# Where the halves of an output weight are made: beside the sample attention, or during the gates and back through DRAM

## The chip, the cores and the metric

The kernel runs on one core of a Trainium2 chip. Five engines work side by side, each from its own queue of instructions: TensorE (PE; its weight loads are listed apart as PEld), VectorE (DVE), ScalarE (ACT), GpSimd (POOL) and SyncE (SP), which here issues nearly all DMA transfers. The metric is the time of one execution on the device in microseconds, the median over runs.

## The reference

One inference step of a two-layer decoder. Layer 0 is a Mamba-2 mixer, layer 1 is multi-head latent attention (MLA), and a norm follows. A prompt of 1024 tokens goes through both. So do 8 sample sequences of 8 new tokens, whose attention also reads 2048 cached positions each, kept in pages of 128 positions that a page table points to. All is in float32. The parts that matter here:

```
def latent_partial(q_lat, q_pe, ckv, kpe, mask):
    s = (jnp.einsum('bqhc,bkc->bhqk', q_lat, ckv.astype(F32))
         + jnp.einsum('bqhr,bkr->bhqk', q_pe.astype(F32), kpe.astype(F32))) * MLA_SCALE
    ...
    m = jnp.max(s, axis=-1)
    p = jnp.exp(s - m[..., None])
    return m, jnp.sum(p, axis=-1), jnp.einsum('bhqk,bkc->bhqc', p, ckv.astype(F32))

def mla_output(o, gate, w_out):
    b, t = o.shape[:2]
    gated = o.reshape(b, t, MLA_WIDTH) * jax.nn.silu(gate.astype(F32))
    return jnp.einsum('bte,ed->btd', gated.astype(gate.dtype), w_out)
...
y_prompt = rms_norm(hp, final_norm_w)
```

`kpe` are the rotary keys of a cached position (32 numbers), `ckv` its latent (256 numbers). `w_out` of the second layer is a matrix of 1024 by 1024; it is the weight that the change is about.

## The kernel before, in words

**Halves.** A float32 product is made of three faster ones: each operand is held as a high half (a copy rounded to the type float32r) and a low half (the operand minus the high half). `split` makes them: a copy on ScalarE, then a subtraction on VectorE or GpSimd (lines 127 to 133).

**The order of the work.** The program is written as Python generators that are stepped in turn. A scheduler then orders each engine's instructions by its own simulated times, so an instruction can be put earlier in its queue than where it is written, as far as its data and buffers allow; `issue_after(x)` puts an instruction behind `x` in the queue of `x`'s engine. In the last two stages the order on TensorE and GpSimd is as written.

**Stages of the second layer.** `mla_in` projects the 1088 tokens. It begins with the gates: eight blocks of 128 columns (`gate_block`), each made of three products (`proj_piece`) of 24 matmuls into one of two PSUM buffers `pj`; ScalarE takes each product out with a SiLU (line 972) and SP stores the block to DRAM. Beside the gates, `gather_kpe` transposes and splits the cached rotary keys and stores the halves to DRAM (two stores of 2 MB, line 1526). Then come keys and latents (`mla_kv`) and queries (`mla_cq`, `mla_q`).

`mla_heads` is the prompt's attention, head by head. During the last head it also starts the sample attention, whose generator `Sample.flow` handles 32 page groups ("pages" from here on), four for each of the eight sequences. One page is 128 rows of 1024 numbers, 512 KB, fetched by GpSimd with an indirect DMA four pages ahead (`load`, line 1625); its rotary rows come in sets for two pages (`load_tk`, three DMAs on SP, line 1618, two buffers). For a page the flow does: two transposes of the page (`turn`, line 1690, with copy and subtraction on lines 1693 and 1694); the scores (seven matmuls, the last one with the rotary rows `tk`); maximum, scale and exponential (lines 1636, 1641, 1644); the transposed probabilities (`turn_p`, line 1732); the halves of the page (line 1703 on ScalarE, line 1705 on GpSimd); and the values (twelve matmuls into `o`), added to the running sum `ac` (line 1753). A new sequence begins with its new tokens (`first_scores`, tiles `P41n`, `pt41n`).

`mla_sample` takes the flow over after the heads, from page 2 on, and beside it runs the output projection of the prompt, `MlaOut.pieces`: eight token tiles, each 48 matmuls with the weight `w5` (line 98). They are stepped from the flow as filler: page 8 does the first twelve matmuls, page 9 the next twelve, and so on (`OUT0`). For each tile an activation tile `og` is loaded from DRAM and split (lines 127 and 131), and a row block `h` is loaded to be added.

**The weight.** It is cut into eight slices of 128 rows, 512 KB each, used in the order `WORD`. Two raw slices are loaded in the last head (`preload`, line 1583), three more when the heads are done, and the last three as raw buffers come free (line 1875). Their halves are made within the flow, at pages 2 to 7 (`WSP`): a copy of 128 by 1024 on ScalarE (line 1883) and four subtractions of 128 by 256 on GpSimd or VectorE by turns (`WENG`, line 1887), each placed behind a named step of the page.

Of the kernel before, what the change touches and what calls it, by code (L numbers as in the profile page):

```python
# [315 lines left out]
def load_w(k, pool, src, nk, ncol, tag, bufs=3, raws=None, rbufs=2, eng=None, sub=0, late=None):  # L316
    raw = load_raw(raws or pool, nk, ncol, rbufs)
    k.nc.sync.dma_start(raw, src.rearrange("(k p) e -> p k e", p=128))
# [646 lines left out]


def gate_block(k, wp, raws, b):
    ws = kslices(load_w(k, wp, k.I["mla_w_in"][0][:, 800 + 128 * b : 928 + 128 * b], 8, 128, "wg", 3, raws, eng=k.nc.gpsimd, sub=4), 8)
    gt = wp.tile([128, T], F32, tag="gt", name=f"gt{b}", bufs=2)

    def ev(ci, t0, n, p):
        k.nc.scalar.activation(gt[:, t0 : t0 + n], p[:, :n], AF.Silu)
# [18 lines left out]
def mla_in(k, right, mid):  # L991
    tc, nc, I = k.tc, k.nc, k.I
    k.g_d = k.dram.tile([8, 128, T], F32, name="g_d")
    with ExitStack() as st:
# [3 lines left out]

        rw = st.enter_context(open_pool(tc, name="rw", bufs=1))
        sg = ExitStack()  # L1000
        wg = sg.enter_context(open_pool(tc, name="wpg", bufs=1))
# [31 lines left out]
        wcq = load_cw(k, wq, rw, 0, 512, "cw")  # L1033
        mla_kv(k, sp, wkv)
        wk.close()
# [5 lines left out]

def mla_kv(k, sp, ws):
    nc, I = k.nc, k.I
# [7 lines left out]
    for i, (t0, m) in enumerate(TILES):  # L1051
# [39 lines left out]
        if i < 8:  # L1091
            kh, kl = k.kT
            split(k, kh[64:96, t0 : t0 + m], kl[64:96, t0 : t0 + m], p[64:96, 256 : 256 + m])


# [363 lines left out]
def mla_heads(k, hd, sm, early, st):  # L1459
# [8 lines left out]
    for h in range(MH):  # L1468
        units, b = [], iter(())
        if h == MH - 2:  # L1470
            early.close()
            hd.rope_queries()
            sm.begin(st, hd.psum)
        if h + 1 < MH:
            a, b = hd.maxpass(h + 1, 0), hd.maxpass(h + 1, 1)
            units += [a] * 4 + [b, a, b, b, b, a] + [b] * 5
        if h + 2 < MH:
            g = hd.prep(h + 2)
            units = merge(units, [g] * hd.units(h + 2))
        if h + 2 == MH:  # L1480
            g = sm.prefetch()
            units[PF:PF] = [g] * 2
            units += [g] * 2
        if h + 1 == MH:
            flow = sm.flow()
            units = [flow] * FLOW
        total, done = len(units), 0
        for t in range(12):
            qc, jb = (0, t) if t < 4 else (1, t - 4)
            held.append((h, qc, jb, *hd.qk(h, qc, jb)))  # L1490
            if t == 0:
                step(turn)
                turn = b
            while done < total * (t + 1) // 12:
                step(units[done])
                done += 1
            if h + 1 == MH and t == 0:
                sm.preload()
            if len(held) > LEAD:
                hd.pv(*held.pop(0))  # L1500
# [44 lines left out]
class Sample:  # L1545
# [28 lines left out]

    def preload(self):
        k = self.k
        self.pre = ExitStack()
        pp = self.pre.enter_context(open_pool(k.tc, name="pre4", bufs=1))
        self.wraw = {}
# [20 lines left out]
    def late_open(self, st):  # L1600
        self.pre.close()
        ap = st.enter_context(open_pool(self.k.tc, name="ap4", bufs=1))
# [9 lines left out]
    def load_tk(self, n):  # L1612
        k, nc = self.k, self.k.nc
        tk = self.ep.tile([96, 4, 256], F32R, tag="tk", name=f"tk{n}", bufs=2)
        for j in range(3):
            src = k.kpe_d[j % 2][:, :, 128 * n : 128 * n + 256].rearrange("r c x -> c r x")
            with k.tc.issue_after(k.lastq.ins):
                nc.sync.dma_start(tk[32 * j : 32 * j + 32].bitcast(F32), src)
        for j in range(2):
# [13 lines left out]
    def softmax(self, name, s, n, old):  # L1633
# [6 lines left out]
        else:  # L1640
            self.nmi = nc.vector.tensor_scalar(nm, mx, -SCALE, old, op0=ALU.mult, op1=ALU.min)
        P = self.sp.tile([128, n], F32, tag=f"P4{n}", name=f"P4{name}", bufs=2)
# [42 lines left out]
    def turn(self, n, c):  # L1685
# [6 lines left out]
        tl = self.ep.tile([128, 512], F32R, tag=f"cTl{c}", name=f"cTl{n}_{c}", bufs=2)  # L1692
        a = nc.scalar.copy(th, pt)
        b = nc.vector.tensor_tensor(tl, pt, th.bitcast(F32), op=ALU.subtract)
        if self.out:
            self.out.pins = a, b
        self.cT[n, c] = (th, tl)
# [85 lines left out]
    def flow(self):  # L1783
        N = len(self.items)
        for n in range(-1, N + 1):
# [9 lines left out]
            if t:  # L1795
                self.turn(n + 1, 1)
                yield
            parts = [WORD[WSP.index(n) + x] for x in range(WSP.count(n))] if out else []
            for kk in parts:
                out.weight_split(kk, 0)  # L1800
            if 0 <= n < N:
                self.scores(n)
                self.weigh(n)
            if parts:
                out.pins = out.pins[0], self.nmi
            for kk in parts:
                out.weight_split(kk, 1)
            if n % 4 == 3 and t:
# [19 lines left out]
            if out:  # L1828
                if n in MORE:
                    next(out.fill, None)  # L1830
                if n + 1 == OUT0[0]:
                    next(out.fill)
                    self.k.nc.sync.dma_start(out.fw, self.k.I["final_norm_w"].partition_broadcast(128))
            yield


def mla_sample(k, sm, flow):
    with ExitStack() as st:
        psum = st.enter_context(open_pool(k.tc, name="ps4", bufs=1, space=PS))
        out = MlaOut(k, st, psum)  # L1840
        sm.open(st, psum, out)
        out.raw = sm.wraw
        for kk in WORD[2:5]:
            out.weight(kk)
        out.fill = fill = out.pieces(range(8))
        next(fill)
        for _ in flow:
            if not hasattr(sm, "accT") and not any(kk in out.raw for kk in WORD[:2]):
                sm.late_open(st)
        last = None  # L1850
# [11 lines left out]
class MlaOut:  # L1862
    def __init__(self, k, st, psum):
        tc, nc, I = k.tc, k.nc, k.I
# [3 lines left out]
        self.fw = sp.tile([128, D], F32, name="fw")  # L1868
        self.raw = {}
        self.ws = [[self.wp.tile([128, D], F32R, name=f"w5{x}{kk}", bufs=1) for x in "hl"] for kk in range(8)]  # L1870

    def weight(self, kk):
        k, nc, wp = self.k, self.k.nc, self.wp
        self.raw[kk] = self.sp.tile([128, D], F32, tag="h5", name=f"w5r{kk}", bufs=3)
        WQ(nc).dma_start(self.raw[kk], k.I["mla_w_out"][0][kk * 128 : kk * 128 + 128])

    def weight_split(self, kk, half):
        hi, lo = self.ws[kk]
        raw = self.raw[kk]
        nc, x = self.k.nc, WENG[WORD.index(kk)]  # L1880
        if not half:
            with self.k.tc.issue_after(self.pins[0].ins):
                nc.scalar.copy(hi, raw)
        for a in range(2 * half, 2 * half + 2):
            s = slice(256 * a, 256 * a + 256)
            with self.k.tc.issue_after(self.pins[1].ins):
                (nc.gpsimd if x & 2 else nc.vector).tensor_tensor(lo[:, s], raw[:, s], hi[:, s].bitcast(F32),
                                                                  op=ALU.subtract)
        if half:
            del self.raw[kk]  # L1890
            if 2 <= WORD.index(kk) < 5:
                self.weight(WORD[WORD.index(kk) + 3])

    def pieces(self, tiles, src=None):
        k, nc, sp, ws = self.k, self.k.nc, self.sp, self.ws

        def load(i):
# [15 lines left out]
        for n, i in enumerate(tiles):  # L1913
            t0, m = TILES[i]
            oh, ol, _, o2 = queue.pop(0)
            h = sp.tile([128, D], F32, tag="h5", name=f"h5{i}", bufs=3)
            nc.sync.dma_start(h[:m], k.h_d[t0 : t0 + m])
            if n + 1 < len(tiles):
# [5 lines left out]
            for hf, c in enumerate(cs):  # L1924
# [3 lines left out]
                for j, _ in enumerate(mm_tok(nc, p, m, nw, [  # L1928
                        (oh[:, kk], ol[:, kk], o2[:, kk], ws[kk][0][:, c], ws[kk][1][:, c]) for kk in WORD])):
                    if j == (7 if src else 11) and nw == 512:  # L1930
# [138 lines left out]
```

## Time and profile before

| | us |
|---|---|
| three runs | 1940.17, 1943.87, 1943.55 |
| median | 1943.55 |
| the profiled execution, its own time | 1941.21 |
| its span, first to last instruction | 1939.4 |
| TensorE busy | 1895.6 |
| VectorE / ScalarE / GpSimd busy | 1192.2 / 1109.9 / 837.5 |
| DMA moved | 202.02 MB, 104 GB/s on the mean |

The time is the slowest core's, and there is one core. Busy times come from one profiled execution; the 1.8 us between its time and its span lie around the first and last instruction. "Busy" for TensorE is modelled and says that a matmul was under way, not that it ran at full rate: the granted clock is a column of its own, 1.00 when nothing is held back. In the names of rows, `out<-in` are the program's tiles; `w5p`, `w5r` are raw slices of the weight, `w5h`, `w5l` its halves.

### The profile page before, as it was taken

Reading aid. Unit: us, or ns where it says so; the run is one execution under the profiler, and the core shown is the slowest. Engines: PE = TensorE matmul, PEld = TensorE weight load, DVE = VectorE, ACT = ScalarE, POOL = GpSimd, SP = SyncE. Lnnn points to the kernel's source line nnn. Section 1 sums busy time; section 2 is a strip of 40 time slices with the busy share of each in tenths; the row PEclk is TensorE's granted clock in tenths of the full one; section 3 lists DMA queues with packets and bytes.
Section 4 is the critical chain, followed back from the end, with each engine's and each line's share of the span. In section 5 each row is a group of like instructions: output and inputs, shape, how many; then the busy total and the mean of one; then the engine's idle time right before and its main releaser. Section 6 shows DMA issues by size and latency. Waiting matters only on the chain.

```text
span 1939.4 us, 33638 instructions
## 1 busy us (share of the span) xinstructions
PE 1895.6 (98%) x12023; PEld 1730.3 (89%) x12023; DVE 1192.2 (61%) x2501; ACT 1109.9 (57%) x2535; POOL 837.5 (43%) x1122
## 2 busy tenths in 40 slices
PE   9999999999999999899999999999999999899998
PEld 7999999999999999788787998898888888788887
DVE  5567666656666666765533104476887888766674
ACT  6467666666666676732214314336777777855552
POOL 2446565555655555443003212103443334764551
PEclk9999999999999999999999999999999999989999
DMA  5123323332323332544433333133111112654431
GB/s 168 47 72 89 98 82 94 83 108 85 97 81 96 86 93 88 193 157 159 179 116 118 123 152 94 56 107 96 47 51 41 51 41 59 215 167 155 156 128 39
DMA packets 181087, 202.02 MB, mean 104 GB/s; under 512 B 18828, under 2 KB 147608, under 8 KB 180536
## 3 DMA queue, kind: packets, MB, share of 16 engines
q1 hardware_dynamic: 175864, 180.08, 30.1%
q0 software_dynamic: 4976, 19.66, 3.0%
q8 instruction: 95, 1.56, 0.3%
q14 instruction: 72, 0.59, 0.1%
q10 hardware_dynamic: 80, 0.13, 0.0%
HBM read 146.52 MB, written 53.28 MB: 103 GB/s over the span
## 4 chain that ended last, share of the span: by engine, by line
PE 88%; DVE 3%; DMA 3%; ACT 3%; issue 1%; POOL 1%; SPq 0%; POOLq 0%; DVEq 0%; ACTq 0%
PE pj L86 21%; PE pz L98 9%; PE pq L98 6%; PE pob L98 5%; PE p L98 5%; PE poa L98 4%; PE py L636 3%; PE sc L86 3%; PE o L86 2%; PE sc L1369 2%; PE o L1432 2%; PE o L1434 2%; PE st L1401 2%; PE st L1402 2%; PE st L1403 2%; PE o L1433 2%
## 5 line engine op out<-in xcount | busy, mean ns | idle before, releaser
L86 PE MATMUL pj<-xh,wih 128*128 128x384 f32 (+1 forms) x768 | 254.2, 335 | 0.9 <-ACT xh L273 0.5
L86 PE MATMUL pj<-xl,wih 128*128 128x384 f32 (+1 forms) x768 | 254.0, 331 | 0.0
L86 PE MATMUL pj<-xh,wil 128*128 128x384 f32 (+1 forms) x768 | 253.2, 330 | 0.0
L1415 POOL TENSOR_TENSOR tl<-P,th 128x384 fp32r<-128x384 f32 (+1 forms) x96 | 90.6, 944 | 232.5 <-ACT P L1413 190.9
L526 DVE SCALAR_TENSOR_TENSOR acc<-raw,vec,acc 128x1112 f32<-128x1112 f32 x96 | 141.6, 1476 | 25.9 <-ACT acc L522 24.9
L86 PEld LDWEIGHTS pj<-xh,wih 128*128 128x128 f32 x768 | 143.9, 188 | 2.5 <-ACT xh L273 1.1
L86 PEld LDWEIGHTS pj<-xl,wih 128*128 128x128 f32 x768 | 144.5, 188 | 1.0
L86 PEld LDWEIGHTS pj<-xh,wil 128*128 128x128 f32 x768 | 144.4, 188 | 0.5
L98 PE MATMUL pz<-wih,xh 128*128 128x256 f32 x504 | 142.9, 287 | 0.9 <-ACT z L567 0.8
L98 PE MATMUL pz<-wil,xh 128*128 128x256 f32 (+1 forms) x504 | 140.4, 285 | 0.9 <-DVE wil L133 0.9
L1412 ACT ACTIVATE th<-st 128x512 fp32r<-128x512 f32 x192 | 94.6, 493 | 66.0 <-PE st L1408 50.3
L631 ACT ACTIVATE M<-M,tok 128x128 f32<-128x128 f32 (+1 forms) x288 | 91.0, 386 | 67.2 <-DVE M L628 66.9
L98 PE MATMUL pz<-wih,xl 128*128 128x256 f32 x448 | 128.2, 286 | 0.0
L1705 POOL TENSOR_TENSOR kvl<-pgr,kvh 128x256 fp32r<-128x256 f32 x128 | 96.5, 781 | 60.5 <-ACT kvh L1703 60.3
L98 PEld LDWEIGHTS pz<-wih,xh 128*128 128x128 f32 x504 | 96.0, 190 | 2.0 <-ACT z L567 1.3
L98 PEld LDWEIGHTS pz<-wil,xh 128*128 128x128 f32 (+1 forms) x504 | 92.7, 184 | 1.7 <-DVE wil L133 1.1
L1413 ACT ACTIVATE P<-st 128x512 f32<-128x512 f32 x192 | 93.5, 487 | 0.0
L628 DVE TENSOR_TENSOR M<-M,negu 128x512 f32<-128x512 f32 x64 | 53.2, 831 | 65.5 <-DMA M<-acs_d 65.1
L613 POOL TENSOR_TENSOR xdd<-xsT,tok 128x256 f32<-128x256 f32 x64 | 50.4, 788 | 84.1 <-ACT xsT L599 84.0
L133 DVE TENSOR_TENSOR wil<-wraw,wih 128x512 fp32r<-128x512 f32 x88 | 72.0, 825 | 23.6 <-ACT wih L127 20.4
L98 PEld LDWEIGHTS pz<-wih,xl 128*128 128x128 f32 x448 | 85.3, 190 | 0.1
L1415 DVE TENSOR_TENSOR tl<-P,th 128x512 fp32r<-128x512 f32 x96 | 70.7, 737 | 18.9 <-ACT P L1413 18.7
(832 smaller groups left out, 6299.0 us busy)
## 6 DMA issues: line engine op xcount, KB each, us to landing
wraw<-in_ssd_w_in SPq DMA_DIRECT2D x92, 256.0 KB
M<-acs_d SPq DMA_DIRECT2D x64, 256.0 KB
s<-in_state_ssm SPq DMA_DIRECT2D x32, 256.0 KB
y_d<-y SPq DMA_DIRECT2D x64, 128.0 KB
out_s_ssm<-s SPq DMA_DIRECT2D x32, 256.0 KB
wraw<-in_ssd_w_out SPq DMA_DIRECT2D x12, 512.0 KB
q_d<-qt SPq DMA_DIRECT2D x32, 192.0 KB
qp<-q_d SPq DMA_DIRECT2D x8, 768.0 KB
```

The costliest lines, as they stand in the source:

```text
L86: nc.tensor.matmul(out, a, b, start=(i == 0), stop=(i == n - 1))
L98: nc.tensor.matmul(o, a, b, start=(j == 0), stop=(j == len(ops) - 1))
L133: return (eng or nc.vector).tensor_tensor(lo, src, hi.bitcast(F32), op=ALU.subtract)
L526: last = nc.vector.scalar_tensor_tensor(acc, raw[:, j : j + n], k.convw[j][:, blk : blk + 1], acc, op0=ALU.mult, op1=ALU.add)
L613: nc.gpsimd.tensor_tensor(v3(xdd), v3(xsT), hb(2), op=ALU.mult)
L628: nc.vector.tensor_tensor(M[:m, :, :m], M[:m, :, :m], (k.negs if smp else k.negu)[:m, :m].unsqueeze(1).to_broadcast([m, 4, m]), op=ALU.add)
L631: nc.scalar.activation(M[:m, h, :m], M[:m, h, :m], AF.Exp, bias=tk[:, 0, 4 * g + h : 4 * g + h + 1])
L636: nc.tensor.matmul(py[:m, h * 64 : h * 64 + 64], M[:m, h, :m], xsT[:m, h * 64 : h * 64 + 64], start=True, stop=True)
L1412: nc.scalar.activation(th[:, :n], ps[:, :n], AF.Exp, scale=SCALE)
L1413: nc.scalar.activation(P[:, :n], ps[:, :n], AF.Exp, scale=SCALE)
L1415: eng.tensor_tensor(tl[:, :n], P[:, :n], th[:, :n].bitcast(F32), op=ALU.subtract)
L1705: nc.gpsimd.tensor_tensor(rl[:, j], raw[:, j], rh[:, j].bitcast(F32), op=ALU.subtract)
```

## The change

The halves are no longer made in the flow. A new generator, `stage_out`, makes them in sixteen pieces (half a slice each: 128 rows by 512 columns): it loads a piece, copies it on ScalarE, subtracts on VectorE in place, and stores both halves side by side to a new DRAM tensor `w5_d`. It is stepped once for each gate product of blocks 2 to 7 but the first, and again in the loop of `mla_kv`. Each piece's load is put behind the newest weight load in SP's queue (`k.lastload`, set in `load_w`).

In the last head, `preload` reads the halves of two slices (`NPW`), 1 MB each, in place of two raw slices; they stay where they are, so the tiles of `late_open` are opened at once beside them. The other six are read at pages 2 to 7, one each, 1 MB, straight into the tiles that the matmuls use, each put behind the newest load of rotary rows (`lasttk`). The loads of the final norm's row (`fw`), of `h`, and of all `og` tiles but the first are put behind `lasttk` too. The matmuls are the same.

```diff
-WSP = (2, 3, 4, 4, 5, 6, 6, 7)
-WENG = (2, 0, 2, 0, 2, 0, 2, 0)
+NPW = 2
+WSP = (2, 3, 4, 5, 6, 7)
...
+def stage_out(k, pool):
+    nc = k.nc
+    k.w5_d = k.dram.tile([8, 128, 2, D], F32, name="w5_d")
+    for n in range(16):
+        kk, s = WORD[n // 2], slice(512 * (n % 2), 512 * (n % 2) + 512)
+        t = pool.tile([128, 2, 512], F32, tag="w5s", name=f"w5s{n}", bufs=3)
+        with k.tc.issue_after(k.lastload.ins):
+            nc.sync.dma_start(t[:, 1], k.I["mla_w_out"][0][kk * 128 : kk * 128 + 128, s])
+        nc.scalar.copy(t[:, 0].bitcast(F32R), t[:, 1])
+        nc.vector.tensor_tensor(t[:, 1].bitcast(F32R), t[:, 1], t[:, 0], op=ALU.subtract)
+        nc.sync.dma_start(k.w5_d[kk][:, :, s], t)
+        yield
...
-        gates = (None for b in range(2, 8) for _ in gate_block(k, wg, rw, b))
+        def gate_steps():
+            for b in range(2, 8):
+                for ci, _ in enumerate(gate_block(k, wg, rw, b)):
+                    if b > 2 or ci:
+                        next(stage, None)
+                    yield
+
+        gates = gate_steps()
...
-    def preload(self):
...
-        for kk in WORD[:2]:
-            self.wraw[kk] = pp.tile([128, D], F32, name=f"w5p{kk}")
+        for kk in WORD[:NPW]:
+            self.ws[kk] = pp.tile([128, 2, D], F32R, name=f"w5{kk}")
             with k.tc.issue_after(k.lastq.ins):
-                k.nc.sync.dma_start(self.wraw[kk], k.I["mla_w_out"][0][kk * 128 : kk * 128 + 128])
+                k.nc.sync.dma_start(self.ws[kk].bitcast(F32), k.w5_d[kk])
...
-            parts = [WORD[WSP.index(n) + x] for x in range(WSP.count(n))] if out else []
-            for kk in parts:
-                out.weight_split(kk, 0)
+            if out and n >= 0:
+                out.weights(n)
             if 0 <= n < N:
                 self.scores(n)
                 self.weigh(n)
-            if parts:
-                out.pins = out.pins[0], self.nmi
-            for kk in parts:
-                out.weight_split(kk, 1)
...
-                    self.k.nc.sync.dma_start(out.fw, self.k.I["final_norm_w"].partition_broadcast(128))
+                    with self.k.tc.issue_after(self.lasttk.ins):
+                        self.k.nc.sync.dma_start(out.fw, self.k.I["final_norm_w"].partition_broadcast(128))
...
+    def weights(self, n):
+        k = self.k
+        for x in range(WSP.count(n)):
+            kk = WORD[NPW + WSP.index(n) + x]
+            with k.tc.issue_after(k.sm.lasttk.ins):
+                WQ(k.nc).dma_start(self.ws[kk].bitcast(F32), k.w5_d[kk])
...
-                nc.sync.dma_start(g, k.og_d[:, :, t0 : t0 + m].rearrange("b p t -> p b t"))
+                with k.tc.issue_after(k.sm.lasttk.ins) if i else nullcontext():
+                    nc.sync.dma_start(g, k.og_d[:, :, t0 : t0 + m].rearrange("b p t -> p b t"))
...
-            nc.sync.dma_start(h[:m], k.h_d[t0 : t0 + m])
+            with k.tc.issue_after(k.sm.lasttk.ins):
+                nc.sync.dma_start(h[:m], k.h_d[t0 : t0 + m])
```

More of the change, by code (lines that the diff above doesn't have):

```diff
@@ L999, in mla_in @@
         rw = st.enter_context(open_pool(tc, name="rw", bufs=1))
+        stage = stage_out(k, st.enter_context(open_pool(tc, name="w5s", bufs=1)))
         sg = ExitStack()
@@ L1033, in mla_in @@
         wcq = load_cw(k, wq, rw, 0, 512, "cw")
-        mla_kv(k, sp, wkv)
+        mla_kv(k, sp, wkv, stage)
         wk.close()
@@ L1039, in mla_in, with mla_kv @@
         mla_cq(k, sp, wcq)
-def mla_kv(k, sp, ws):
+def mla_kv(k, sp, ws, stage):
     nc, I = k.nc, k.I
@@ L1093, in mla_kv @@
             split(k, kh[64:96, t0 : t0 + m], kl[64:96, t0 : t0 + m], p[64:96, 256 : 256 + m])
+        next(stage, None)
 def mla_cq(k, sp, ws):
@@ L1497, in mla_heads @@
             if h + 1 == MH and t == 0:
-                sm.preload()
+                sm.preload(st)
             if len(held) > LEAD:
@@ L1573, in pt, with preload @@
         return self.psum.tile([128, 512], F32, tag=tag, name=name, bufs=bufs)
-    def preload(self):
+    def preload(self, st):
         k = self.k
-        self.pre = ExitStack()
-        pp = self.pre.enter_context(open_pool(k.tc, name="pre4", bufs=1))
-        self.wraw = {}
-        for kk in WORD[:2]:
-            self.wraw[kk] = pp.tile([128, D], F32, name=f"w5p{kk}")
+        pp = st.enter_context(open_pool(k.tc, name="pre4", bufs=1))
+        self.ws = {}
+        for kk in WORD[:NPW]:
+            self.ws[kk] = pp.tile([128, 2, D], F32R, name=f"w5{kk}")
             with k.tc.issue_after(k.lastq.ins):
-                k.nc.sync.dma_start(self.wraw[kk], k.I["mla_w_out"][0][kk * 128 : kk * 128 + 128])
+                k.nc.sync.dma_start(self.ws[kk].bitcast(F32), k.w5_d[kk])
     def load_cn(self, b):
@@ L1617, in load_tk @@
             with k.tc.issue_after(k.lastq.ins):
-                nc.sync.dma_start(tk[32 * j : 32 * j + 32].bitcast(F32), src)
+                self.lasttk = nc.sync.dma_start(tk[32 * j : 32 * j + 32].bitcast(F32), src)
         for j in range(2):
@@ L1692, in turn @@
         tl = self.ep.tile([128, 512], F32R, tag=f"cTl{c}", name=f"cTl{n}_{c}", bufs=2)
[L1693 to L1696, printed above, removed]
+        split(k, th, tl, pt)
         self.cT[n, c] = (th, tl)
@@ L1839, in mla_sample @@
         psum = st.enter_context(open_pool(k.tc, name="ps4", bufs=1, space=PS))
-        out = MlaOut(k, st, psum)
+        out = MlaOut(k, st, psum, sm)
         sm.open(st, psum, out)
-        out.raw = sm.wraw
-        for kk in WORD[2:5]:
-            out.weight(kk)
+        sm.late_open(st)
+        k.sm = sm
         out.fill = fill = out.pieces(range(8))
         next(fill)
-        for _ in flow:
-            if not hasattr(sm, "accT") and not any(kk in out.raw for kk in WORD[:2]):
-                sm.late_open(st)
+        drain(flow)
         last = None
@@ L1862, with __init__ @@
 class MlaOut:
-    def __init__(self, k, st, psum):
+    def __init__(self, k, st, psum, sm):
         tc, nc, I = k.tc, k.nc, k.I
@@ L1868, in __init__ @@
         self.fw = sp.tile([128, D], F32, name="fw")
[L1869 to L1892, printed above, removed]
+        self.ws = dict(sm.ws)
+        for kk in WORD[NPW:]:
+            self.ws[kk] = self.wp.tile([128, 2, D], F32R, name=f"w5{kk}", bufs=1)
+    def weights(self, n):
[4 more added lines that the diff above has]
+                WQ(k.nc).dma_start(self.ws[kk].bitcast(F32), k.w5_d[kk])
     def pieces(self, tiles, src=None):
@@ L1928, in pieces @@
                 for j, _ in enumerate(mm_tok(nc, p, m, nw, [
-                        (oh[:, kk], ol[:, kk], o2[:, kk], ws[kk][0][:, c], ws[kk][1][:, c]) for kk in WORD])):
+                        (oh[:, kk], ol[:, kk], o2[:, kk], ws[kk][:, 0, c], ws[kk][:, 1, c]) for kk in WORD])):
                     if j == (7 if src else 11) and nw == 512:
```

5 lines of the change are left out of this document (2 added, 3 removed).

## The prediction

> **What bounds the kernel now.** I read the page first, then the busy time by 10 us windows over the last third, then the waits of TensorE, then the timeline of the stretch those two single out, and last the DMA issues. On the page TensorE is busy nearly all the time:
>
> ```profile
> span 1939.4 us, 33638 instructions
> PE 1895.6 (98%) x12023; PEld 1730.3 (89%) x12023; DVE 1192.2 (61%) x2501; ACT 1109.9 (57%) x2535; POOL 837.5 (43%) x1122
> ```
>
> Only 43.8 us (1939.4 - 1895.6) can be had without removing matmuls, and this change removes none. The windows show where a good part of it lies. Columns: window, length, busy us (and instructions) of PE, PEld, DVE, ACT, POOL, granted clock, DMA share, GB/s.
>
> ```profile
> 1670.00:1680.00 10.00, 9.22 (x63) 7.94 (x62) 5.41 (x11) 7.95 (x15) 7.07 (x10) 1.00 0.52 167
> 1680.00:1690.00 10.00, 6.17 (x44) 5.50 (x45) 10.00 (x24) 7.98 (x15) 6.13 (x8) 1.00 1.09 330
> 1690.00:1700.00 10.00, 5.60 (x29) 4.16 (x28) 9.96 (x16) 4.63 (x11) 9.81 (x12) 0.85 0.72 242
> 1700.00:1710.00 10.00, 7.77 (x45) 7.22 (x45) 6.78 (x13) 7.38 (x14) 9.74 (x14) 0.81 0.74 223
> 1710.00:1720.00 10.00, 10.00 (x58) 8.79 (x58) 7.65 (x21) 6.67 (x14) 6.43 (x9) 0.83 0.70 227
> ```
>
> TensorE idles 0.78 + 3.83 + 4.40 + 2.23 = 11.2 us in these 50 us, while VectorE, then GpSimd, is full; after it the clock drops. The waits of TensorE from 1400 us on name whom it waits for (total, times, longest, us):
>
> ```profile
> PE pt41n L1671 <- ACT P41n L1644: 3.2, 1, 3.2
> PE o L86 <- DVE ac L1753: 3.2, 1, 3.2
> PE pt L1732 <- ACT P L1644: 2.7, 2, 2.2
> PE o L86 <- DVE pTl L133: 2.2, 2, 1.3
> ```
>
> Those are the page loop's own softmax and accumulator steps, late in their queues. The timeline shows what stands ahead of them: two casts of the weight's high halves just before that exponential, and on VectorE a weight split and an activation split just before that accumulator.
>
> ```profile
> 1671.47 0.48 PE L86 MATMUL sc<-cTh,qlh 128*128 128x512 f32 x1
> ...
> 1676.82 0.48 PE L86 MATMUL sc<-cTh,qlh 128*128 128x512 f32 x1
> ...
> 1685.87 2.00 ACT L1883 CAST w5h<-w5r 128x1024 fp32r<-128x1024 f32 x2
> ...
> 1689.71 3.12 DVE L1887 TENSOR_TENSOR w5l<-w5r,w5h 128x256 fp32r<-128x256 f32 x4
> ...
> 1692.76 3.55 DVE L131 TENSOR_TENSOR ol<-og,oh 128x256 fp32r<-128x256 f32 x4
> ...
> 1717.36 0.48 PE L86 MATMUL sc<-cTh,qlh 128*128 128x512 f32 x1
> ```
>
> The first row is the start of page 2's scores, the second of page 3's, the last of page 8's. So six pages take 45.9 us, 7.6 each, while page 2 alone took 5.35.
>
> **The change, part by part.** *Splits removed from pages 2 to 7.*
>
> ```profile
> L1887 POOL TENSOR_TENSOR w5l<-w5r,w5h 128x256 fp32r<-128x256 f32 x12 | 9.6, 831 | 0.1
> L1887 DVE TENSOR_TENSOR w5l<-w5r,w5h 128x256 fp32r<-128x256 f32 x12 | 8.2, 726 | 0.0
> ...
> L1883 ACT CAST w5h<-w5r 128x1024 fp32r<-128x1024 f32 x6 | 6.2, 1051 | 0.2 <-DMA w5r<-in_mla_w_out 0.2
> ```
>
> These are six of eight slices; scaled by 8/6 the eight cost GpSimd 12.8, VectorE 10.9 and ScalarE 8.3 us. Of the 34.4 us that VectorE is busy in the windows from 1680 to 1720 some 23.5 are left; it is full no more. The second activation tile's split (the 3.55 us row) leaves too: its load is now tied behind the rotary rows of page 10, so it comes after page 7. What remains is the first tile's split. All of the 11.2 us of waits then loses its cause, but something is late next: page 2, with almost none of the new splits in it, took 5.35 us, and the waits row for `pt L1732` (2.7 in two, longest 2.2) leaves a first wait of 0.5 us there, for the exponential behind the scores. I leave 0.4 us a page, 2.5 over six. Gain of this term: 11.2 - 2.5 = 8.7.
>
> *The clock.* The three windows with 0.85, 0.81 and 0.83, weighted by PE's busy time in them, lose 5.60 x 0.15 + 7.77 x 0.19 + 10.00 x 0.17 = 4.0 us. The drop stands right behind the waits, so I count all 4.0 as gained. Cross-check: 45.9 - 11.2 - 4.0 = 30.7 us, 5.1 a page, against page 2's 5.35 with its wait.
>
> The Trainium skill, page "TensorE: Matmul & The Clock Gate", section "Part 1: The HAM clock gate", says that the clock falls to half after at least one idle window of about 3.4 us, in a window that runs free. The longest wait here is 3.2 us and the clock did fall, so the waits rows go a little further than that rule; by its letter the drop would have another cause and stay.
>
> *Slices read back.* Two slices of 1 MB (halves together) go into the preload in place of 0.5 MB each, ahead of page 2's rotary rows in SP's queue; the other six are read one per page, 1 MB each, behind the newest rotary rows. SP issues as many DMAs as before.
>
> ```profile
> 1675.58 1.49 SPq L1875 DMA_DIRECT2D w5r<-in_mla_w_out  x3
> ```
> ```profile
> tk<-kpe_dh SPq DMA_DIRECT2D x32, 128.0 KB
> og<-og_d SPq DMA_DIRECT2D x8, 512.0 KB
> ...
> w5r<-in_mla_w_out SPq DMA_DIRECT2D x6, 512.0 KB
> ```
> ```profile
> 1682.32 7.28 DMA tk<-kpe_dl
> ```
>
> The first is when the heads' last store lets the weight loads go; then come sizes; then how long a set of rotary rows took to land behind three slices, two og tiles and the final norm's row (3.1 MB). The last weight is first used in page 9's fill step: 1671.5 + 7 x 5.1 = 1707.2, plus about 5 us of scores and fill ahead, say 1712. From 1675.6 to there, 36 us, the queues must bring six slices (6.3 MB), one og tile (0.5), two sets of rotary rows (0.8) and five pages (2.6): 10.2 MB, 283 GB/s. What they can do: 330 at a share of 1.09 is 303 GB/s at full share, 242 at 0.72 is 336. It fits by 7 to 19%. Rows for page 6, behind three slices and og 0 (3.7 MB, against 3.1 before), land some 1.7 us later than the 1689.6 of the quoted row, 1691.3; they are the last matmul of page 6's scores, 1671.5 + 4 x 5.1 + 1.4 = 1693.3. Cover of 2 us. Bounds: 0 by 303 GB/s or more; at the 223 of the slowest window 45.7 us, so 10 late. I take 1.0, near the lower end, since the slow windows had a share of 0.72 to 0.74 and were not full.
>
> *Halves made in the gates.* Sixteen pieces, one per gate product from the second on: a 256 KB load, a 128x512 copy on ScalarE, a subtraction on VectorE, a 512 KB store, so 32 more DMAs on SP. (The calls left in the key/value loop find nothing to do: seventeen gate steps exhaust sixteen pieces.)
>
> ```profile
> 1060.00:1156.00 96.00, 94.84 (x589) 92.32 (x588) 13.09 (x25) 25.47 (x48) 19.37 (x27) 1.00 0.38 136
> ```
> ```profile
> 1100.00:1110.00 10.00, 10.00 (x66) 9.96 (x65) 0.69 (x1) 2.76 (x6) 2.83 (x4) 1.00 0.14 57
> ```
> ```profile
> L972 ACT ACTIVATE gt<-pj 128x384 f32<-128x384 f32 (+1 forms) x20 | 9.4, 469 | 50.0 <-PE pj L86 41.5 <-issue 8.5
> ...
> L127 ACT CAST kpeh<-kpt 128x512 fp32r<-128x512 f32 x8 | 4.6, 585 | 0.0
> ```
> ```profile
> L133 DVE TENSOR_TENSOR kpel<-kpt,kpeh 128x512 fp32r<-128x512 f32 x8 | 5.4, 691 | 41.4 <-ACT kpeh L127 41.4
> ```
> ```profile
> h_d<-xrb POOLq DMA_DIRECT2D x1, 256.0 KB, 4.2
> ```
>
> 16 x 0.585 = 9.4 us on ScalarE and 16 x 0.691 = 11.1 on VectorE, in 96 us where they are busy 25.5 and 13.1: hidden. DMA: 12.6 MB in some 70 us is 180 GB/s beside 136, near 316: hidden only if nothing PE needs stands behind it. PE's step is 24 x 10/66 = 3.6 us, with two PSUM buffers. The exposed price: each piece's copy stands in ScalarE's queue ahead of a gate evacuation, and SP's store waits for the subtraction with the next loads behind it. Bounds: 0, or, with every copy waiting for its load as long as the one 256 KB transfer with a landing (4.2), 16 x (4.2 + 0.585 + 0.469 - 3.6) = 26. No gain is possible, as PE's matmuls there are unchanged. Three buffers let loads run ahead, so I take 0.5.
>
> **Sum.** 8.7 + 4.0 - 1.0 - 0.5 = 11.2 us. Against the profiled execution's 1941.2 us that is 1930.0; it stood 2.3 us under the median of the three runs, 1943.55, so I say 1932.5 for the median.
>
> **Rivals.** *Rotary rows and slices late.* For it: the chain through this stretch already counts the quoted 7.28 us landing. Against: VectorE had no idle time there. At 249 GB/s, the mean over 1675 to 1712 before,
>
> ```profile
> 1675.00:1712.00 37.00, 25.82 (x152) 22.16 (x151) 30.80 (x59) 26.85 (x49) 30.32 (x39) 0.89 0.80 249
> ```
>
> 10.2 MB take 41 us, 5 late, 4 more than summed, and 1.7 for a halved clock window of 3.4 us: 1938.2.
>
> *The waits stay.* The first og split and the exponential behind the scores take the freed places, and half the idle (5.6) and clock (2.0) remain: 1932.5 + 5.6 + 2.0 - 2.5 = 1937.6, up to 1941 if the halves removed were not the last to end. For it: the 3.55 us row is not a weight split. Against: GpSimd's and VectorE's full windows are those of the weight splits.
>
> *The clock drop has its own cause.* It falls in these windows whatever PE waits for: 1936.5. Against: the drop begins in the very windows that hold the waits, after 1.00 in the two before.
>
> *Slower: ScalarE waits in the gates.* The price above, with every copy waiting 4.2 us, is 26: 1958. It decides from a wait of 3.3 us per copy: 16 x (3.3 + 1.05 - 3.6) = 12, the whole gain. For it: the rotary cache's two 2 MB stores stand in the same queue late in the gates. Against: ScalarE idles 50 us for PE there.
>
> **Numbers.** Likeliest, with its own range 1929 to 1937: 0.55. Rows late 0.14 (half of it within 0.2%, spreading to 1943), waits stay 0.08, clock 0.05, slower 0.18. Within 0.2% (3.9 us, about what the runs can tell from nothing) also takes the upper part of the second rival. Faster 0.71, same 0.11, slower 0.18. Range 1928 to 1944: it leaves out the slower case and little else.
>
> **What would show it.** Right: windows 1670 to 1710 with PE at 9.5 or more, clock 1.00, page 8 starting near 1703 to 1705, no w5 casts there. Rows late: TensorE waiting at `sc` for `tk`, or at L98 for `w5`. Slower: `pj` of the gates waiting for ScalarE, and page 2 starting later than 1671.5 by more than 2 us, which would make the prediction wrong.

## The result, and the profile after

The change makes no difference: 1943.76 us (median of 14 executions) against 1943.00 for the kernel before on the same chip, a ratio of 1.0004 (95% interval 0.9993 to 1.0015). The forecast was 1932.5. The profiled execution of the changed kernel took 1944.85 us, its span is 1943.1.

From the page of the changed kernel, span and busy time of TensorE:

```profile
span 1943.1 us, 33685 instructions
PE 1897.2 (98%) x12023; PEld 1729.7 (89%) x12023; DVE 1196.4 (62%) x2501; ACT 1108.6 (57%) x2543; POOL 824.7 (42%) x1106
```

The windows of the changed kernel, the same 10 us ones that the prediction showed and one more (window, length, busy us of PE, PEld, DVE, ACT, POOL, granted clock, DMA share, GB/s):

```profile
1680.00:1690.00 10.00, 7.33 (x54) 6.54 (x55) 6.49 (x18) 5.85 (x12) 5.77 (x7) 1.00 0.79 281
1690.00:1700.00 10.00, 9.12 (x62) 7.82 (x61) 7.59 (x17) 6.27 (x15) 6.99 (x10) 1.00 1.07 378
1700.00:1710.00 10.00, 8.02 (x56) 6.98 (x54) 5.74 (x12) 6.62 (x14) 7.34 (x10) 1.00 1.03 346
1710.00:1720.00 10.00, 10.00 (x69) 8.77 (x67) 5.20 (x14) 3.89 (x10) 4.90 (x6) 1.00 1.06 320
1720.00:1730.00 10.00, 7.12 (x23) 5.73 (x23) 5.40 (x12) 4.95 (x10) 3.89 (x5) 0.66 0.17 53
```

No engine but TensorE is full any more, as forecast (VectorE had 10.00 and 9.96 before), and the clock holds at 1.00 up to 1720. But idle time is left, the DMA engines are now the full ones from 1690 to 1720, and the clock drop has moved to 1720. The starts of page 0, 2, 8 and 10 on the timeline of the changed kernel, and of page 0 and 10 on that of the kernel before (its pages 2 and 8 are in the prediction):

```profile
1660.84 0.39 PE L86 MATMUL sc<-cTh,qlh 128*128 128x512 f32 x1
...
1676.64 0.48 PE L86 MATMUL sc<-cTh,qlh 128*128 128x512 f32 x1
...
1713.43 0.47 PE L86 MATMUL sc<-cTh,qlh 128*128 128x512 f32 x1
...
1734.51 0.47 PE L86 MATMUL sc<-cTh,qlh 128*128 128x512 f32 x1
```
```profile
1655.68 0.39 PE L86 MATMUL sc<-cTh,qlh 128*128 128x512 f32 x1
...
1732.58 0.48 PE L86 MATMUL sc<-cTh,qlh 128*128 128x512 f32 x1
```

Pages 2 to 8 take 36.8 us where they took 45.9: 9.1 gained. Pages 8 to 10 take 21.1 instead of 15.2: 5.9 lost. Page 0 starts 5.2 later, and from page 10 on another 1.8 are lost (1943.1 - 1734.5 = 208.6 against 206.8; experiment 2 below gives 1.0 of it back). Together that is, to rounding, the 3.7 us between the two spans. 1.3 of the 5.2 are there at 1042 us, where the gates begin and ahead of any work that was changed, so we take them for scatter of one execution.

The waits of TensorE in the changed kernel, 1670 to 1745 us (total, times, longest, us):

```profile
PE pt L1751 <- ACT P L1666: 6.4, 4, 2.9
PE ct L1712 <- DMA pgr<-in_cache_ckv,ptidx: 2.0, 1, 2.0
```

6.4 us are again for the exponential `P`. What held it is on ScalarE's timeline, ahead of page 4 and at page 8 (in brackets, the idle time before a row and what ended it):

```profile
1686.96 1.04 ACT L127 CAST oh<-og 128x1024 fp32r<-128x1024 f32 x1 [2.26 <-issue]
1687.91 0.58 ACT L127 CAST cTh<-ct 128x512 fp32r<-128x512 f32 x1
1688.95 0.69 ACT L1666 ACTIVATE P<-sc,nm 128x512 f32<-128x512 f32 x1 [0.46 <-DVE nm L1663]
...
1715.45 0.26 ACT L1695 COPY pn<-pt42n 8x128 f32<-8x128 f32 x1
1721.80 1.04 ACT L127 CAST oh<-og 128x1024 fp32r<-128x1024 f32 x1 [6.09 <-DMA og<-og_d]
1722.75 0.68 ACT L1666 ACTIVATE P<-sc,nm 128x512 f32<-128x512 f32 x1
```

Both times the cast of an activation tile stands ahead of an exponential, and ScalarE sits idle at it, 2.26 and 6.09 us. For the second the profile names the tile's load as what it waits for. For the first it names nothing; the load had been issued 5.5 us before, and in experiments 1, 5 and 9 the same cast starts 5.4 to 5.7 us after that issue, so we read this as a wait for the tile too. VectorE's timeline shows what the exponentials themselves needed, the scaled maximum `nm`:

```profile
1688.03 0.76 DVE L131 TENSOR_TENSOR ol<-og,oh 128x256 fp32r<-128x256 f32 x2 [1.72 <-ACT oh L127]
1688.71 0.21 DVE L1663 TENSOR_SCALAR nm<-mx,nm 128x1 f32<-128x1 f32 x1
...
1716.84 0.20 DVE L1663 TENSOR_SCALAR nm<-mx,nm42n 128x1 f32<-128x1 f32 x1
```

At page 8 it was ready at 1717.0, and the exponential still started only at 1722.75, right behind the cast: here the queue of ScalarE alone held it. Ahead of page 4 the cast held it in two queues: on ScalarE, with one more short cast between, and on VectorE, where `nm` stood behind two subtractions of the same tile and so came last. The Trainium skill, page "Perfetto Trace Analysis", section "Tensor Engine Instruction (MATMUL, LD_WEIGHTS)", says that ScalarE, VectorE and GpSimd work strictly first in, first out; this trace agrees: the exponential of page 8 starts 0.95 us after the cast, at once when its turn comes. SyncE's timeline of the changed kernel shows why the second tile is late, and one more thing far ahead of it:

```profile
1076.76 0.60 SPq L1533 DMA_DIRECT2D kpidx<-in_page_table  x1
...
1682.14 1.69 SPq L1890 DMA_DIRECT2D w<-w_d  x3
...
1684.93 7.52 SPq L1640 DMA_DIRECT2D tk<-kpe_dh  x1
...
1711.93 0.43 SPq L1903 DMA_DIRECT2D og<-og_d  x1
```
```profile
1063.87 0.42 SPq L1509 DMA_DIRECT2D kpidx<-in_page_table  x1
```

The second tile's load, tied behind page 10's rotary rows, is issued at 1711.93 and lands 9.8 us later, when the cast starts. Those rows have two buffers, and SyncE waited 9.1 us for TensorE's scores to free one. Three slices stand ahead of page 6's rotary rows, whose issue alone then takes 7.52 us. And the index load of the rotary gather (the single row is the kernel before's), which the gates' end needs, is issued 12.9 us later than before, behind the weight's pieces.

### The profile page after: what moved, and what is told of

The parts are those of the page before. It is cut to its first block, busy times and chain, and to the rows that moved or that the text cites. A ratio compares the mean times of both kernels' runs of the same rounds, so it can differ in the third digit from the quotient of the medians.

```text
span 1943.1 us, 33685 instructions
## 1 busy us (share of the span) xinstructions
PE 1897.2 (98%) x12023; PEld 1729.7 (89%) x12023; DVE 1196.4 (62%) x2501; ACT 1108.6 (57%) x2543; POOL 824.7 (42%) x1106
## 4 chain that ended last, share of the span: by engine, by line
PE 80%; DMA 7%; ACT 5%; DVE 4%; issue 2%; POOL 2%; SPq 0%; DVEq 0%; POOLq 0%; ACTq 0%
PE pj L86 19%; PE pz L98 9%; PE pq L98 6%; PE pob L98 5%; PE p L98 4%; PE poa L98 4%; PE py L636 2%; PE sc L86 2%; DMA M<-acs_d 2%; PE sc L1393 2%; PE o L1456 2%; PE o L1458 2%; PE st L1425 2%; PE o L86 2%; PE st L1426 2%
## 5 line engine op out<-in xcount | busy, mean ns | idle before, releaser
L98 PE MATMUL p<-w,oh 128*128 128x512 f32 (+3 forms) x304 | 89.1, 387 | 0.6 <-DVE h L1932 0.6
```

The source lines that it names most:

```text
L98: nc.tensor.matmul(o, a, b, start=(j == 0), stop=(j == len(ops) - 1))
```

## The experiments

All were timed in five rounds beside the kernel before, whose medians were 1942.7 (experiments 1, 2, 4 and 5), 1942.5 (3, 6, 7 and 8) and 1942.1 us (9 to 11). A ratio is to that kernel. Differences of medians across these groups carry at least the 0.9 us between the lowest of these and the 1943.0 above, and each trace is of one execution, up to 3.8 us from its kernel's median (experiment 1: 1942.05 us). "Half clock" is a granted clock of 0.50.

**1. The tie of the second activation tile undone.**

```diff
-                with k.tc.issue_after(k.sm.lasttk.ins) if i else nullcontext():
+                if True:
                     nc.sync.dma_start(g, k.og_d[...])
```

> The changed kernel with one part undone: og loads are no longer tied behind the rotary rows. Theory A (ScalarE's head of queue: the cast of the second og tile stands ahead of page 8's exponential and waits 6.1 us for a load issued at 1711.9): the wait of 2.88 us on TensorE and the half clock behind it (3.4 us) go, about 6 us, so 1937 to 1939 against 1943. Theory B (the queues are full from 1683 to 1722, and whatever is put earlier delays something else): pages and rotary rows come later by the same amount, no change, 1942 to 1945.

Measured 1938.26 us, ratio 0.9982 (0.9967 to 0.9997). TensorE's waits, 1670 to 1745 us:

```profile
PE pt L1751 <- ACT P L1666: 4.4, 3, 3.1
PE o L86 <- DVE pTl L133: 1.6, 1, 1.6
```

The 2.9 us wait at page 9 is gone; that of page 4, for the first tile's cast, is now the longest, 3.1. So the tie cost some 5.5 us of the medians, 4.3 by the ratios: the one wait and the half clock behind it, by our reading, though this trace has a half clock of its own, 3.4 us from 1704 on.

**2. The casts behind the exponential.** The ties stay. `lastexp` is the newest exponential.

```diff
+        self.lastexp = nc.scalar.activation(P[:, :n], s, AF.Exp, ...)
...
+        with k.tc.issue_after(k.sm.lastexp.ins):
             split(k, *queue[0][:3], parts=4 if tiles[0] == 0 else 0)
...
+                        with k.tc.issue_after(k.sm.lastexp.ins):
                             split(k, *queue[0][:3], ...)
```

> The changed kernel, with ScalarE's cast of each og tile put behind the newest exponential in its queue; loads stay as they are. Theory A: the waits of 2.24 us (page 4) and 2.88 us (page 9) on TensorE for the exponential go, with the half clock behind the second: 7 to 9 us, 1935 to 1937. Theory B: the exponential is no longer late but the pages are (1.98 us at page 7 grows), no more than 3 us gained, 1940 to 1943.

Measured 1936.22 us, ratio 0.9967 (0.9956 to 0.9978): 7.5 us of the medians for the order of a few instructions on ScalarE. The first tile's cast now starts at 1710.45, behind page 7's exponential, and waits for nothing. The waits of TensorE, 1670 to 1745 us, are now for rotary rows:

```profile
PE sc L86 <- DMA tk<-kpe_dh: 2.4, 2, 1.8
PE pt L1751 <- ACT P L1666: 0.6, 2, 0.4
```

and the queue row that stands for their lateness is SyncE's, behind three slices:

```profile
1684.13 9.16 SPq L1640 DMA_DIRECT2D tk<-kpe_dh  x1
```

**3. The kernel before with the same casts edit** (casts behind the newest exponential, weight halves still made in the pages).

> The kernel before (weight splits in the pages, no pieces), with one edit: the ScalarE casts of the activation tiles stand behind the newest exponential. Theory (what held the pages up was the work on VectorE, GpSimd and ScalarE of the weight's own splits): little moves, 1940 to 1943. Rival (the order of the activation casts alone made the waits, and the change to the weight was not needed): 1936 to 1938, as good as the change with the same edit.

Measured 1941.63 us, ratio 0.9996 (0.9984 to 1.0008): nothing that can be told apart. TensorE's waits there:

```profile
PE pt L1732 <- ACT P L1644: 5.9, 5, 2.8
PE pt41n L1671 <- ACT P41n L1644: 1.4, 1, 1.4
```

The exponential is held up by the weight's own splits when the activation casts are out of its way (in this trace a weight cast that waits 1.99 us for its slice stands ahead of it before the 2.8 us wait), and by the activation casts when the splits are. Each cause covers the other: the change alone gives +0.8 us, the order of the casts alone -0.9, both -6.5.

**4. The pieces alone.** The kernel before, with the sixteen pieces made and stored in the gates, and nothing reading them.

> The kernel before, plus the sixteen pieces in the gates with their stores; nothing reads what they store, and the flow splits the weight as before. Theory A (the gates cost what the offset between the two profiles grows by from 1042 to 1345 us, 3.9 us): 1946 to 1948 against 1943. Rival (that offset is the scatter of single executions): 1943 to 1944.

Measured 1945.07 us, ratio 1.0010 (0.9998 to 1.0023): 2.4 us, between the two ranges expected, with an interval that still holds "no difference". In this trace the wait for the gathered rows is 0.2 us, though the index load comes as late as in the changed kernel (1077.8 us).

**5. Half of the bytes.** The changed kernel reads only the high halves of the six slices; the low halves are left out of the output product.

> The changed kernel, reading only the high halves of the six slices at pages 2 to 7 (512 KB each, half the bytes); the matmuls use the high half for both, so the low halves of these six are left out of the result. Theory A: the second og tile is still behind the rows of page 10, so most of the 2.88 us wait stays if the rows are what it waits for, and goes if the queue was merely full. Theory B (full queues are the cause of all three waits): TensorE waits under 2 us from page 2 to page 10, clock 1.00, 1934 to 1938.

Measured 1939.50 us, ratio 0.9983 (0.9972 to 0.9994). Waits of TensorE, 1670 to 1745 us:

```profile
PE pt L1751 <- ACT P L1666: 4.7, 4, 3.0
```

With 3 MB less the second tile's cast still stands ahead of page 8's exponential, but waits 1.68 us instead of 6.09, and TensorE no longer waits for it; page 4's wait stays, with a half clock behind it. So the full queue made the second wait, as the second half of Theory A has it, but not the first, against Theory B.

**6. Slices after the page's rotary rows** (on top of 2).

```diff
-            if out and n >= 0:
-                out.weights(n)
...
                 (the page's rotary rows, load_tk)
+            if out and n >= 0:
+                out.weights(n)
```

> The change with the casts of the activation tiles behind the newest exponential (1936.2 us), and in addition each page's slice reads are issued after the rotary rows of that page instead of before them, so that two slices, not three, stand ahead of page 6's rows. Theory (the queue's order sets when the rows land): the two waits of the scores for the rows (1.85 at 1700.4, 0.52 at 1712.2 us) go, and with them the half clock behind the first (3.4 us at half, 1.7 us lost): 4.1 us, less 1 to 2 for the next late transfer, 1932.5 to 1934. Rival (the DMA engines are full from 1683 to 1722 us and only the order of lateness changes): a page, an og tile or a slice is late in its place, a wait of 1 to 3 us stands at another matmul, 1935.5 to 1938.

Measured 1934.04 us, ratio 0.9951 (0.9936 to 0.9966). The waits for rotary rows are gone, and the half clock behind the first; the longest wait from 1670 to 1745 is 0.8. The median is 2.2 us lower than that of 2, but the two intervals overlap.

**7. The index load ahead of the pieces** (on top of 2).

```diff
-        with k.tc.issue_after(k.lastload.ins):
+        with k.tc.issue_after(k.lastload.ins), k.tc.issue_after(k.slotload.ins):
             nc.sync.dma_start(t[:, 1], k.I["mla_w_out"][0][...])
```

> The change with the casts behind the newest exponential (1936.2 us), and in addition the pieces' first loads stay behind the load of the page table's slots, so that the index load for the rotary gather is issued ahead of all pieces, as before the change (1063.9 instead of 1076.8 us). Theory (the pieces cost what they push back in SP's queue): the wait of 1.0 us for the gathered rows and part of the 1.1 us wait at the query projection go, 1934.3 to 1935.4, and page 0 starts 1 to 2 us earlier than 1659.7. Rival (the later start of page 0 comes from ahead of the gates and from the preload): no change, 1935.8 to 1936.6.

Measured 1933.57 us, ratio 0.9951 (0.9931 to 0.9970): 2.6 us off the median, 0.7 more than the theory's best, with an interval that overlaps that of 2. The theory is not borne out. The wait for the gathered rows is gone, but from the start of the gates to page 0 the kernel takes 613.9 us, as 2 does; waits of 0.9 and 0.7 us at the query projection stand in its place. In the pages TensorE waits 0.4 us for rotary rows where 2 waited 2.4, and the half clock of 2 (3.4 us, so 1.7 lost) is not there, though nothing was changed there. These alone come to 3.7 us, so the 2.6 cannot be put down to the index.

**8. Both** (2, 6 and 7).

> The change with the casts behind the newest exponential, the slice reads after the page's rotary rows, and the pieces behind the page table's slots. Theory: the two gains add, 1930.5 to 1933.0. Rival (the same full DMA engines, the same start of page 0): 1935 to 1937.

Measured 1932.86 us, ratio 0.9952 (0.9932 to 0.9971): faster than both kernels, but not told apart from 2, 6 or 7 by their intervals; whether the gains of 6 and 7 add is open. Windows of this kernel (columns as above), and TensorE's waits, 1670 to 1745 us:

```profile
1680.00:1690.00 10.00, 9.75 (x68) 8.76 (x69) 6.62 (x18) 6.66 (x17) 7.41 (x11) 1.00 0.94 347
1690.00:1700.00 10.00, 9.84 (x64) 8.23 (x63) 7.31 (x15) 6.86 (x15) 7.50 (x10) 1.00 1.06 374
1700.00:1710.00 10.00, 9.54 (x65) 8.10 (x64) 6.05 (x17) 7.65 (x17) 6.95 (x10) 1.00 1.03 342
1710.00:1720.00 10.00, 9.21 (x50) 7.17 (x49) 8.07 (x16) 4.17 (x11) 5.76 (x8) 1.00 1.05 305
```
```profile
PE p L98 <- DVE ol L131: 0.8, 1, 0.8
PE pt L1751 <- ACT P L1666: 0.6, 2, 0.4
PE pt L1751 <- issue: 0.5, 1, 0.5
```

The DMA engines are as full as in the changed kernel, and TensorE hardly waits: fullness alone was not the trouble, order was. The page starts of this kernel, 2 and 8:

```profile
1675.62 0.48 PE L86 MATMUL sc<-cTh,qlh 128*128 128x512 f32 x1
...
1707.38 0.48 PE L86 MATMUL sc<-cTh,qlh 128*128 128x512 f32 x1
```

Six pages in 31.8 us. The prediction's cross-check was 30.7; its sum, which leaves 2.5 us of waits in them, makes 33.2.

**9. Both orders of DMAs, but not the casts** (6 and 7 without 2).

> The two orders of DMAs mended (slices after the page's rotary rows, pieces behind the page table's slots), but the casts of the activation tiles left where the change has them, ahead of the exponential. Theory (the casts cost what their edit gave, 7.5 us of 1943.8, and the queue orders the rest): 1938 to 1940.5, with the waits of 2.2 us in page 4 and of nearly 3 us at page 9 still there. Rival (with less DMA in the way the activation tiles land in time and the casts no longer wait): 1933 to 1935.

Measured 1938.79 us, ratio 0.9982 (0.9972 to 0.9992). The wait of page 4 stays, and the half clock with it (waits, then the window that holds it):

```profile
PE pt L1751 <- ACT P L1666: 4.7, 4, 2.9
```
```profile
1680.00:1690.00 10.00, 7.05 (x42) 6.25 (x41) 5.36 (x17) 4.79 (x10) 3.59 (x6) 0.83 1.04 386
```

The expected wait near page 9 was not there, and not because the tile came sooner: it lands 10.1 us after its issue, as late as before. The scheduler has put its cast behind page 8's exponential this time:

```profile
1713.06 0.69 ACT L1666 ACTIVATE P<-sc,nm 128x512 f32<-128x512 f32 x1 [1.44 <-DVE nm L1663]
...
1717.97 1.05 ACT L127 CAST oh<-og 128x1024 fp32r<-128x1024 f32 x1 [1.22 <-DMA og<-og_d]
```

So this kernel is not the order of DMAs alone: the edits to SyncE's queue moved one of the two casts as well. Of the 10.9 us between the changed kernel and 8, it gets 5.0 and experiment 2 gets 7.5; what the order of DMAs is worth by itself is not shown.

**10. All orders mended, without the pieces** (8 without the sixteen pieces; slices of the same size are read from the rotary cache's halves, so the weight is other numbers).

> The change with all three orders mended (casts behind the exponential, slices after the page's rotary rows, pieces behind the page table's slots: 1932.9 us), without the sixteen pieces: nothing is staged, and the slices of the same size are read from the rotary cache's own halves instead, so the weight of the output product is other numbers; the pages' work and bytes stay. It prices what the pieces still cost. Theory (they lie beside other work once the index load stands ahead of them; 2.6 us of small waits at the query projection, none there before, are all they cost): 1929.5 to 1931.5. Rival (they are free, and those waits are scatter of the order of work): 1932.5 to 1933.5. Rival (they cost as much as the staging alone did, 2.4 us, and more through the bytes): under 1929.5.

Measured 1932.88 us, ratio 0.9944 (0.9930 to 0.9958); 8 had 0.9952. The median is where the first rival had it. Once the index load goes ahead of them, the pieces cost 0 to 3 us: the medians say nothing, the ratios 1.5 (their intervals overlap), and the traces 1.5 to 3.2 from the start of the gates to page 0 (611.7 to 611.9 us in three kernels without pieces, 613.4 to 614.9 in four with the index first, 613.9 to 616.3 in six with the pieces first). That is as far as it is settled.

**11. All orders mended and the second tile's tie undone.**

> All three orders mended (1932.9 us), and the load of the second activation tile no longer tied behind the rotary rows of page 10, as in the kernel before. Theory (with the casts behind the exponential the tie no longer costs anything but the 0.8 us wait for that tile's low half at page 9): 1931.5 to 1933. Rival (0.5 MB more ahead of the slices and rows makes one of these late): 1934 to 1936.

Measured 1933.82 us, ratio 0.9952 (0.9937 to 0.9967): not told apart from 8. The wait for the tile's low half is gone, and the rotary rows are late in its place, as the rival had it, by 1.8 us in two waits, 1.4 the longest. With the casts behind the exponential, undoing the tie gains nothing.

## Why the prediction was wrong, point by point

**"What remains is the first tile's split. All of the 11.2 us of waits then loses its cause."** This step failed, in the first term of the sum (8.7 us) and with it the second (4.0). It read the weight's own splits ahead of the late exponential and accumulator as the only cause, and they hid a second one: the activation casts, which the scheduler puts ahead of an exponential and which wait for a load. The first tile's split was seen and put at nothing: the 2.5 us left in the term are short waits for the exponential behind the scores, not a place in a queue that stands 2.26 us idle. The second tile's was counted as gone, "so it comes after page 7". It did come after page 7, and the sum ended there: at page 8, ahead of that page's exponential, it waited 6.09 us for a load that the change itself had tied behind other work, and pages 8 to 10 lost 5.9 us. Experiment 2 takes the casts from ahead of the exponential, edits no DMA, and gains 7.5 us. Experiment 3 shows that the weight splits were a cause as well, as the prediction had it: without the change the same edit gives nothing.

**The clock.** That the drop follows the waits holds: it is at 1720 in the changed kernel (0.66 in that window), with and behind the 2.9 us wait, and in the runs where no wait of the pages exceeds 1.4 us (6, 7, 8, 10, 11) no window from 1670 to 1750 is below 1.00. So the rival in which the drop has its own cause falls. The 4.0 us were right in kind and were not gained, since the waits were not.

**Slices read back, 1.0 us.** Size and sign were near, the reasoning was not. The prediction asked for 10.2 MB in 36 us and had a capacity of 303 to 336 GB/s. In those 36 us, from the heads' last store on, the changed kernel moved more, and faster:

```profile
DMA packets 5369, 12.26 MB, mean 340 GB/s; under 512 B 1426, under 2 KB 3597, under 8 KB 4598
```

Left out of the 10.2 were the second activation tile, the final norm's row, the rows of `h`, one gate block, a sixth page and a third set of rotary rows. The volume fitted nevertheless; what came late came by its place in SP's queue. With the casts mended the rows for page 6 were 1.85 us late, and two instead of three slices ahead of them (experiment 6) took that wait away. The 2 us cover that the prediction gave these rows was thus gone as soon as the pages ran at the speed that it forecast.

**Halves made in the gates, 0.5 us.** The pieces' own work was sized well: forecast were 9.4 us on ScalarE and 11.1 on VectorE, and the groups of the changed kernel, 1041 to 1160 us, show

```profile
L976 DVE TENSOR_TENSOR w5s<-w5s 128x512 fp32r<-128x512 f32 x16 | 13.3, 836 | 12.3 <-ACT w5s L975 12.3
...
L975 ACT CAST w5s<-w5s 128x512 fp32r<-128x512 f32 x16 | 9.8, 616 | 7.3 <-DMA w5s<-in_mla_w_out 4.9 <-issue 2.4
```

The copies did wait for their loads, but 7.3 us in all (4.9 of it named as a load) instead of the slower rival's 67 (16 times 4.2), and TensorE's waits for the gates did not grow. The term was too small all the same, as far as can be told. The prediction said "hidden only if nothing PE needs stands behind it" and did not go through SP's queue to see that something does. The index load stood behind the pieces, so the gathered rotary rows came late, the first of these rows; the second is at the query projection (TensorE's waits of the changed kernel, 1040 to 1100 and 1100 to 1340 us; the kernel before has neither):

```profile
PE kpt L1544 <- DMA kprows<-in_cache_kpe,kpidx: 1.0, 1, 1.0
...
PE pq L98 <- ACT qt L1161: 1.3, 2, 1.1
```

Experiment 4 puts the whole at 2.4 us, not clear of nothing. Experiment 7 takes the first wait away without a shorter way to page 0, so the path by which the pieces cost more than 0.5 us, if they do, stays open.

**The rivals.** The nearest was "The waits stay", with 0.08: it named the first activation split and the exponential, and its 1937.6 to 1941 still lay below the result, since it had neither the second tile nor the index. The prediction's own argument against it, that the full windows are those of the weight splits, was true and proved nothing: it showed one cause, not that there was only one. That 1943.76 lies just inside the stated range is no merit: its upper end, 1944, was drawn at the time before the change, and "same" had a chance of 0.11. With three orders mended the gain is 9.6 us against 11.2 forecast, at 1932.9 against 1932.5 (the working gives 1930.0 + 2.3 = 1932.3). The size was thus near for the mechanism, and in part by luck, since that kernel has orders mended that the prediction did not price.

## What to carry to other kernels

When work ahead of a late instruction is removed, look at what comes next in that engine's queue and at what each of these waits for: a short cast that waits for a DMA holds everything behind it, and is invisible in busy times. Tying a load behind other transfers also ties whatever consumes it, so the consumer has to move back in its own queue as well. Extra transfers can fit by volume, as 12.26 MB did here in 36 us, and still make something late, since they go through the issuing queue row by row: list what stands behind them there, and who waits for it.

## What was not expected of the hardware

The DMA engines carried more than the windows of the kernel before had let one think. In the 10 us from 1683 to 1693 us of the changed kernel, with 1 MB slices under way:

```profile
DMA packets 1551, 3.92 MB, mean 392 GB/s; under 512 B 64, under 2 KB 1025, under 8 KB 1241
```

The Trainium skill, page "DMA: Bandwidth & Descriptors", section "Where 436 GB/s comes from", says that transfers between HBM and SBUF are bound by HBM at about 358 GB/s for one core, the 716 of a stack divided by two cores; here, with one core at work, 392 were moved over 10 us, so the measurement decides, and the bound does not hold for this core in this stretch.

The clock drops behind waits much shorter than its own low stretch. In windows of 1 us it goes from 1.00 (1721 to 1722 us in the changed kernel) to 0.50 and back to 1.00 (1730 to 1731):

```profile
1725.00:1726.00 1.00, 1.00 (x5) 0.90 (x4) 1.00 (x2) 1.00 (x4) 1.00 (x2) 0.50 0.00 0
```

Longest waits and drops in the pages: half clock with or right behind 1.65 (experiment 1) and 1.85 us (2), as with 2.77 (3), 2.88 (the change), 2.94 (9) and 3.04 (5); none with 2.24 and 1.98 (the change) or 3.12 (1). The half clock lasted 3.4 us, or 6.8 in the changed kernel. So the length of one wait does not decide; what does, these runs don't show. The rule of the Trainium skill that the prediction weighed (page "TensorE: Matmul & The Clock Gate", section "Part 1: The HAM clock gate", at least one idle window of about 3.4 us) does not agree with the two short ones.

An issue on SyncE is not always cheap: that of the first rotary rows took 7.52 us behind three slices (9.16 in experiment 2), where the same line takes 0.3 to 0.6 in the changed kernel's other issues around it, and everything behind it in the queue waits as long.
